# Measuring out projection work by each step's vector work, with a shorter DRAM round trip and a refilled weight ring

## The chip, the cores and the metric

The kernel runs on one core of a Trainium2 chip. The core has TensorE (matmuls; weight loads are shown on a line of their own, PEld), VectorE (DVE), ScalarE (ACT), GpSimd (POOL) and SyncE (SP), which run beside each other and wait for one another by semaphores. In this kernel SP and POOL mainly issue DMA transfers. The metric is the device time of one execution in microseconds; of several runs the median is given.

## The reference

One decoder layer for one sequence of 2048 tokens, 1024 wide, all in float32:

```python
h = rmsnorm(x, norm1_w)
proj = h @ w_in                                # 1024 x 3840
q_raw, f_raw, i_raw, g_raw = split(proj[..., :2048], 4)
o_hg = hgrn2(...)                              # 4 heads of 128: gated linear recurrence
rw_p = proj[..., 2048:]
rw_p = rw_p + (token_shift(rw_p) - rw_p) * mu
r, k, v, wd, ad, gd = split(rw_p, ...)
# RWKV-7, 8 heads of 64; the state S is 64 x 64 for each head:
#   sa = S a_t ;  S = S diag(w_t) + sa b_t^T + v_t k_t^T ;  y_t = S r_t
o_rw = groupnorm(y) * ln_w + ln_b + bonus, gated by g
x = x + concat([o_hg, o_rw], -1) @ w_out       # 1024 x 1024
u = causal_depthwise_conv3(rmsnorm(x, norm2_w) @ w_up) + conv_b     # 1024 x 5632
x = x + (silu(u[:2816]) * u[2816:]) @ w_down
return rmsnorm(x, final_norm_w)
```

Both recurrences run over the 2048 tokens. The kernel computes them in chunks of 64 tokens.

## The kernel before

**Arithmetic.** A large product is three matmuls on a value split into a high and a low part: high x high, high x low, low x high (`mm3`, L257 to L261). Each is 128x128 times 128x512. Splitting a weight is a cast on ScalarE (L243) and a subtraction on VectorE (L244).

**Two phases.** Phase 1 (`phase1`, L263 to L1085) has the input projection, both recurrences and the output projection of the first three of the four blocks of 512 tokens. Phase 2 (from L1088) has the output projection of the last block (accumulators `wacc`), then the FFN, whose two products are built from sums of blocks. The last matmuls of phase 1 and the first of phase 2 meet at what is called the seam. Phase 2 begins with loads on SP: three of convolution rows (`crow`, L1144 to L1146), then w_out and the recurrences' result `oT`, through the helper at L1153.

**Phase 1 is three streams.** Each is a Python generator that issues instructions and yields.

- `rw_stream`: RWKV-7 in eight super-steps (`rw_super`, L630 to L921), each of two head pairs over 512 tokens. In order: decays and keys; the masked products M (L706 to L709), a part of which makes a first round trip through DRAM (Ed, E, L715 to L725) that turns it so that each 32x32 triangle lies in one partition; transposes and `lv` (L757); the inversion of these triangles by elimination, 31 dependent steps of a multiply and an add on VectorE (L776, L778); a second round trip (L781 to L795), Ti and its transpose TiT to DRAM (T0d, T1d), then back as TZ and TTs; the matmuls that combine the halves, z (L802), z2 (L815), q (L828), g (L852, with adds at L855 and L858 that write AR), x (L868) and y (L875); the scan of the state, eight dependent steps of four small matmuls (L886) and a multiply on VectorE (L888); the output (L896 to L916) and the store of `oT` (L919).
- `hg_stream`: HGRN2 in sixteen units (`hg_unit`, L924 to L1046), among them the matmuls at L970 and L1012.
- `dense`: the list of projection jobs (L499 to L616). A "P" job is 128 columns for 512 tokens: eight k-steps of three matmuls with accumulator `pj`, each booked at 648 ns. There are 30 for each block. An "O" job is the output block of one of the blocks 0 to 2 (`out_block`, L367 to L401): four quarters of eight k-tiles; each k-tile loads and splits one 128x512 weight of w_out (`woraw`, on the POOL queue) and uses it for two booked units of 680 ns. Other jobs load and transpose rows (T, N) or make sums for phase 2 (E, W). The order is P of blocks 0 and 1, O of block 0, P of block 2, O of block 1, P of block 3, O of block 2.

**The pace.** The loop at L1078 takes one step of each recurrence and then calls `fill`, which draws projection units until the booked time is spent. That is a tick. TICK is 2000 ns for every tick, whatever the two steps hold:

```python
        while any(alive.values()):
            for key, g in (("r", rw_), ("h", hg_)):
                ...
            fill(TICK)
```

A unit that has to wait for a recurrence yields None, and the tick's credit is dropped. After the second round trip the RWKV stream yields twice (L796), so that two ticks of projection lie between it and L802. The list scheduler of the tile framework then places each engine's instructions by its own estimates and by the order in which they were issued.

**The weight ring.** Split weights lie in the buffers `wh` and `wl`, four of each. One P job takes two of each (k-tiles 0 to 3 and 4 to 7), one k-tile of an O job takes one of each. `load(i)` (L545) loads the weights of job i: for the first block raw from w_in, with split, and stores both parts to DRAM (Win); later blocks load the stored parts straight into wh and wl, by four DMAs on POOL (L558). At the head of each P job `load(i + 1)` (L596) issues the next job's load, whatever stands between the two.

Of the kernel before, what the change touches and what calls it, by code (L numbers as in the profile page):

```python
# [7 lines left out]
F32 = mybir.dt.float32  # L8
# [10 lines left out]
P = 128  # L19
T = 2048  # L20
D = 1024
KD = D // P
# [3 lines left out]
NFF = FF // P  # L26
TICK = 2000.0
NEG_C = -0.6065306597126334
# [30 lines left out]


@with_exitstack
def tile_layer(ctx, tc, consts, x, norm1_w, w_in, hg_lb_logits, hg_norm_w, rw_shift_mu, rw_w0, rw_w2,
# [3 lines left out]
    nc = tc.nc  # L66
    V, S, TE = nc.vector, nc.scalar, nc.tensor
    dma = nc.sync.dma_start
# [40 lines left out]
    def act(out_, in_, func, **kw):  # L109

        want = tables.get(func)
        if want is not None and want != tab["now"]:
            pre = S.preload_act_table_set(want)
            for u_ in tab["uses"]:
                tc.add_manual_dep(pre.ins, u_.ins.name, NOSYNC, reason="table order")
            tab.update(now=want, pre=pre, uses=[])
        i_ = S.activation(out_, in_, func, **kw)  # L117
        if want is not None:
            tc.add_manual_dep(i_.ins, tab["pre"].ins.name, NOSYNC, reason="table order")
            tab["uses"].append(i_)  # L120
        return i_
# [13 lines left out]
    with tc.tile_pool(name="vp", bufs=1, reuse_waits="tile") as vp, tc.tile_pool(name="ps0", bufs=1, space=PSUM, reuse_waits="tile") as pools["ps"]:  # L135
        rows = vp.tile([P, P], F32, name="rows")
        V.memset(rows, 0.0)
        n = 0
# [124 lines left out]
    def phase1(c1):  # L263
# [102 lines left out]

        def out_block(nb, oh=None, ol=None, then=None):  # L367


            for i2 in range(2):  # L370
                for dh in range(2):
                    accs = [bank("pj") for _ in range(2)]
                    for k in range(KD):
# [16 lines left out]
                        for q in range(2):  # L390
# [4 lines left out]
                            if i2 == 1 and dh == 1 and q == 1:  # L395
                                next_block(then, k)
                            yield 680
                    for q in range(2):
# [4 lines left out]
        rows = {}  # L403
# [95 lines left out]
        def dense():  # L499
# [64 lines left out]
            for n, jb in enumerate(jobs):  # L564
# [14 lines left out]
                if jb[0] in "OW":  # L579
                    while done["rw2"] < 2 * jb[1] + 2 or done["hg"] < 4 * jb[1] + 4:  # L580
                        yield None
                    if jb[0] == "W":
                        jb[2]()
                    else:
                        yield from (out_block(2, *rows["O"]) if jb[1] == 2 else out_block(jb[1], then=jb[1] + 2))
                    continue
# [5 lines left out]
                if i == 0:  # L592
                    next(ahead)
                    next(ahead)
                    constants()
                load(i + 1)  # L596
                i += 1
# [32 lines left out]
        def rw_super(nb, s_):  # L630
# [84 lines left out]
            Ed = dp.tile([64, 32, 32], F32, tag="Ed", name="Ed", bufs=2)  # L715
            T0d = dp.tile([2, 64, 32, 16], F32, tag="T0d", name="T0d", bufs=2)
            T1d = dp.tile([64, 16, 2, 32], F32, tag="T1d", name="T1d", bufs=2)
# [6 lines left out]
            for f in range(2):  # L724
                dma(E[64 * f:64 * f + 64], Ed)  # L725

            KBT = tile_("KBT", [2, 8, P], "KBT")
# [53 lines left out]
            TiT = rp.tile([P, 16, 32], F32, tag="E", name="TiT")  # L781
            dma(T0d.rearrange("f m t c -> (f m) t c"), Ti)
            act(TiT, Ti.rearrange("m a b -> m b a"), AF.Copy)
# [3 lines left out]
            for e in range(2):  # L787
                r0 = er0(e)
                for f in range(2):
                    dma(TZ[r0:r0 + 32, 0].rearrange("p u b h t -> p (u b h) t")[:, :, 16 * f:16 * f + 16],  # L790
                        T0d[f, 32 * e:32 * e + 16].rearrange("m t c -> t m c"))
                for q in range(2):
                    m0 = (e * 2 + q) * 16
                    dma(TTs[r0 + 32 * q:r0 + 32 * q + 32, :, 32 * q:32 * q + 32],
                        T1d[m0:m0 + 16].rearrange("m c f t -> (c f) m t"))  # L795
            for _ in range(2):  # L796
                yield
            z = bank2()
# [278 lines left out]

        while any(alive.values()):  # L1078
            for key, g in (("r", rw_), ("h", hg_)):
                if alive[key]:  # L1080
                    try:
                        next(g)
                    except StopIteration:
                        alive[key] = False
            fill(TICK)  # L1085

# [424 lines left out]
```

## Time and profile before

| | |
|---|---|
| runs | 2757.32, 2753.06, 2752.97 us; median 2753.06 |
| the profiled execution | 2757.5 us, of which the span is 2755.7 |
| mean granted TensorE clock in it | 0.983 |
| busy, share of the span | TensorE 96%, its weight loads 76%, VectorE 69%, ScalarE 49%, GpSimd 13% |
| projection matmuls (pj with wh, wl: 3 x 960) | 404.9, 380.6 and 380.6 us recorded; mean 397 to 422 ns of one |
| DMA | 515.78 MB, 187 GB/s on average |

The span runs from the first to the last record of the core; a part of the execution lies around it. The recorded durations of pipelined matmuls overlap (397 to 422 ns each), so they do not add up to time; how many end in a stretch does.

The lines below come from five views. The shares of the **chain of waits** follow the work that ended last backwards and say which engine or transfer it ran on. A **table by stretch** gives each engine's busy time in a window, with the granted clock, the busy share of the DMA engines and GB/s. A row of the **waits** says which engine and line waited (`PE pj L259`) for which engine and line (`ACT wh L243`), then the sum in us, the count and the longest. A **group** of instructions has a line, engine, operation, output<-input and count, then busy us, mean ns, and the idle time before them with what ended it. A **DMA row** ends with KB of one and the median us from issue to landing.

### The profile page before, as it was taken

What the parts mean: (1) busy time and instruction counts of PE and PEld (TensorE: products, weight loads), DVE (VectorE), ACT (ScalarE), POOL (GpSimd) and SP (SyncE); (2) the same over time, 40 slices, a digit from 0 to 9 for tenths busy, and PEclk for the clock granted to TensorE, in tenths of its full rate; (3) what the DMA queues carried; (4) which work ended last, traced back from release to release, by engine and by line L of the source; (5) the groups of instructions that cost most, each with busy time, mean ns of one, the idle gap of its engine ahead of it and who ended that gap; (6) DMA issues with size and microseconds to landing.
All of it is one profiled execution on the core that took longest, in us unless ns stands there. A gap on an engine that the chain in (4) does not pass through costs nothing.

```text
span 2755.7 us, 47958 instructions
## 1 busy us (share of the span) xinstructions
PE 2647.8 (96%) x18059; PEld 2107.5 (76%) x18059; DVE 1898.6 (69%) x3665; ACT 1350.4 (49%) x2164; POOL 368.3 (13%) x660
## 2 busy tenths in 40 slices
PE   7999999989999999999989999998999999999998
PEld 6777777767777767778667788886888888877887
DVE  4856556565456664657657889988997786667656
ACT  5546443444544444344446755455455555445444
POOL 6433222212321113222100000000000000000000
PEclk9999999999999999999999999999999999999999
DMA  8645544355663546844575367746662224999865
GB/s 301 202 152 166 165 138 131 115 146 173 217 176 104 152 146 203 286 138 123 161 273 160 114 205 258 242 148 218 223 228 77 88 85 144 327 327 313 285 196 184
DMA packets 364285, 515.78 MB, mean 187 GB/s; under 512 B 97311, under 2 KB 193941, under 8 KB 364053
## 3 DMA queue, kind: packets, MB, share of 16 engines
q1 hardware_dynamic: 312113, 343.29, 38.6%
q0 software_dynamic: 51872, 169.41, 18.9%
q8 instruction: 142, 2.33, 0.3%
q14 instruction: 90, 0.74, 0.1%
q10 hardware_dynamic: 68, 0.02, 0.0%
HBM read 375.22 MB, written 137.36 MB: 186 GB/s over the span
## 4 chain that ended last, share of the span: by engine, by line
PE 73%; DMA 8%; DVE 7%; issue 5%; ACT 4%; SPq 1%; POOL 1%; DVEq 0%; ACTq 0%; POOLq 0%
PE pj L259 8%; PE pj L260 7%; PE pj L261 7%; PE ua L261 5%; PE ua L259 5%; PE ua L260 5%; PE ud L259 3%; PE ud L260 3%; PE ud L261 3%; PE da L260 2%; PE da L261 2%; PE da L259 2%; PE hg L970 2%; PE db L259 2%; PE db L261 2%
## 5 line engine op out<-in xcount | busy, mean ns | idle before, releaser
L259 PE MATMUL pj<-hh,wh 128*128 128x512 f32 x960 | 404.9, 422 | 0.7 <-ACT hh L117 0.7
L261 PE MATMUL pj<-hh,wl 128*128 128x512 f32 x960 | 380.6, 397 | 0.0
L260 PE MATMUL pj<-hl,wh 128*128 128x512 f32 x960 | 380.6, 397 | 0.0
L259 PE MATMUL ua<-Bh,uwh 128*128 128x512 f32 x704 | 278.6, 396 | 13.8 <-ACT uwh L243 13.1
L261 PE MATMUL ua<-Bh,uwl 128*128 128x512 f32 x704 | 276.9, 394 | 0.9 <-DVE uwl L244 0.9
L260 PE MATMUL ua<-Bl,uwh 128*128 128x512 f32 x704 | 276.4, 393 | 0.0
L259 PEld LDWEIGHTS pj<-hh,wh 128*128 128x128 f32 x960 | 182.4, 190 | 54.2 <-issue 11.8
L260 PEld LDWEIGHTS pj<-hl,wh 128*128 128x128 f32 x960 | 182.6, 190 | 39.7 <-issue 6.2
L261 PEld LDWEIGHTS pj<-hh,wl 128*128 128x128 f32 x960 | 182.2, 190 | 40.1 <-issue 0.4
L243 ACT CAST uwh<-uraw 128x512 fp32r<-128x512 f32 x220 | 134.8, 618 | 145.9 <-PE ua L260 73.2
L243 ACT CAST dah<-draw 128x512 fp32r<-128x512 f32 x151 | 93.8, 621 | 184.1 <-PE da L260 50.5
L244 DVE TENSOR_TENSOR uwl<-uraw,uwh 128x512 fp32r<-128x512 f32 x220 | 146.7, 684 | 47.5 <-ACT uwh L243 47.3
L244 DVE TENSOR_TENSOR dal<-draw,dah 128x512 fp32r<-128x512 f32 x151 | 104.0, 689 | 107.3 <-ACT dah L243 107.2
L259 PEld LDWEIGHTS ua<-Bh,uwh 128*128 128x128 f32 x704 | 133.6, 190 | 43.1 <-ACT uwh L243 13.7
L261 PEld LDWEIGHTS ua<-Bh,uwl 128*128 128x128 f32 x704 | 133.5, 190 | 30.6 <-DVE uwl L244 2.7
L260 PEld LDWEIGHTS ua<-Bl,uwh 128*128 128x128 f32 x704 | 133.6, 190 | 27.3
L259 PE MATMUL ud<-Bh,uwh 128*128 128x512 f32 x352 | 137.9, 392 | 1.9 <-DVE cv L1362 1.9
L261 PE MATMUL ud<-Bh,uwl 128*128 128x512 f32 x352 | 137.1, 389 | 0.0
L260 PE MATMUL ud<-Bl,uwh 128*128 128x512 f32 x352 | 137.0, 389 | 0.0
L260 PE MATMUL da<-dbl,dah 128*128 128x512 f32 x340 | 133.8, 394 | 0.6 <-DVE dbl L244 0.5
L261 PE MATMUL da<-dbh,dal 128*128 128x512 f32 x340 | 133.3, 392 | 0.0
L259 PE MATMUL da<-dbh,dah 128*128 128x512 f32 x340 | 128.3, 391 | 2.4 <-ACT dbh L243 2.3
(558 smaller groups left out, 6036.7 us busy)
## 6 DMA issues: line engine op xcount, KB each, us to landing
uraw<-in_w_up_dram SPq DMA_DIRECT2D x176, 256.0 KB, 3.3
woraw<-in_w_out_dram POOLq DMA_DIRECT2D x96, 256.0 KB, 3.6
draw<-Sg SPq DMA_DIRECT2D x88, 256.0 KB, 3.1
draw<-Tw SPq DMA_DIRECT2D x88, 256.0 KB, 3.0
gd<-y SPq DMA_DIRECT2D x86, 256.0 KB, 2.9
xt<-x1d SPq DMA_DIRECT2D x32, 512.0 KB, 6.0
draw<-gd SPq DMA_DIRECT2D x63, 256.0 KB, 4.8
draw<-in_w_down_dram SPq DMA_DIRECT2D x63, 256.0 KB, 5.3
```

Source lines behind the costliest of these rows:

```text
L243: S.copy(hi, src)
L244: V.tensor_sub(lo, src, hi.bitcast(F32))
L259: TE.matmul(acc, lh, rh, start=first, stop=False, skip_group_check=skip)
L260: TE.matmul(acc, lh, rl, start=False, stop=False, skip_group_check=skip)
L261: TE.matmul(acc, ll, rh, start=False, stop=last, skip_group_check=skip)
L970: TE.matmul(o, kt[:, t0:t0 + 64], qs, start=True, stop=True, tile_position=(0, e * 64))
```

## The change

1. **Booking.** VectorE's engine object is wrapped (`Metered`): each of its operations adds 150 ns and 1.04 ns for each element of a row of its output to a counter; each ScalarE activation adds half of what it would be on VectorE. Each of the two round trips adds 8000.
2. **Pacing.** A tick's projection work is no longer 2000 ns but 900 ns and 0.45 of what the tick's two steps added to the counter. In place of two yields after the second round trip there is one.
3. **Round trip.** The DRAM buffer of Ti changes its layout, from (half, triangle, row, 16 columns) to (triangle, row, half, 16 columns). Its store becomes two DMAs in place of one, with runs of 64 bytes in DRAM; the loads of TZ become two in place of four. Both are issued ahead of the four loads of TTs, not among them.
4. **Ring.** The load of the next projection's weights is no longer issued at the head of the job ahead of an output block, but in the block, at the third last k-tile of its last quarter.

Lines of the recurrences lie about 30 lower in the new file. A VectorE operation that is called through the wrapper carries the wrapper's line there (L80).

```diff
-TICK = 2000.0
+FLOOR, RATE = 900.0, 0.45
+OP_NS, ELEM_NS, TRIP_NS = 150.0, 1.04, 8000.0
...
+class Metered:
+    def __init__(self, engine):
+        self.engine, self.ns = engine, 0.0
+    def __getattr__(self, name):
+        call = getattr(self.engine, name)
+        def f(out_, *args, **kw):
+            self.ns += OP_NS + ELEM_NS * width(out_)
+            return call(out_, *args, **kw)
+        return f
...
+    V = Metered(nc.vector)
...
+        V.ns += 0.5 * (OP_NS + ELEM_NS * width(out_))
         i_ = S.activation(out_, in_, func, **kw)
...
                             if i2 == 1 and dh == 1 and q == 1:
                                 next_block(then, k)
+                                if k == KD - 3 and last is not None:
+                                    last()
...
-                load(i + 1)
+                kinds = [jb_[0] for jb_ in jobs[n + 1:]]
+                if "O" not in kinds[:kinds.index("P") if "P" in kinds else 0]:
+                    load(i + 1)
...
-            T0d = dp.tile([2, 64, 32, 16], F32, tag="T0d", name="T0d", bufs=2)
+            T0d = dp.tile([64, 32, 2, 16], F32, tag="T0d", name="T0d", bufs=2)
...
             for f in range(2):
                 dma(E[64 * f:64 * f + 64], Ed)
+            V.ns += TRIP_NS
...
-            dma(T0d.rearrange("f m t c -> (f m) t c"), Ti)
+            for f in range(2):
+                dma(T0d[:, :, f, :], Ti[64 * f:64 * f + 64])
...
-                for f in range(2):
-                    dma(TZ[r0:r0 + 32, 0].rearrange("p u b h t -> p (u b h) t")[:, :, 16 * f:16 * f + 16],
-                        T0d[f, 32 * e:32 * e + 16].rearrange("m t c -> t m c"))
+                dma(TZ[r0:r0 + 32, 0].rearrange("p u b h t -> p (u b h) t"),
+                    T0d[32 * e:32 * e + 16].rearrange("m t f c -> t m (f c)"))
+            for e in range(2):
+                r0 = er0(e)
                 for q in range(2):
                     m0 = (e * 2 + q) * 16
                     dma(TTs[r0 + 32 * q:r0 + 32 * q + 32, :, 32 * q:32 * q + 32],
                         T1d[m0:m0 + 16].rearrange("m c f t -> (c f) m t"))
-            for _ in range(2):
-                yield
+            V.ns += TRIP_NS
+            yield
...
         while any(alive.values()):
+            t0 = V.ns
...
-            fill(TICK)
+            fill(FLOOR + RATE * (V.ns - t0))
```

More of the change, by code (lines that the diff above doesn't have):

```diff
@@ L58, in make_consts, with width @@
     return c
+def width(ap):
+    n = 1
+    for d in ap.shape[1:]:
+        n *= d
+    return n
+class Metered:
[7 more added lines that the diff above has]
+        return f
 @with_exitstack
@@ L66, in tile_layer @@
     nc = tc.nc
-    V, S, TE = nc.vector, nc.scalar, nc.tensor
+    S, TE = nc.scalar, nc.tensor
+    V = Metered(nc.vector)
     dma = nc.sync.dma_start
@@ L365, in mark, with out_block @@
             return f
-        def out_block(nb, oh=None, ol=None, then=None):
+        def out_block(nb, oh=None, ol=None, then=None, last=None):
             for i2 in range(2):
@@ L584, in dense @@
                     else:
-                        yield from (out_block(2, *rows["O"]) if jb[1] == 2 else out_block(jb[1], then=jb[1] + 2))
+                        yield from (out_block(2, *rows["O"]) if jb[1] == 2 else
+                                    out_block(jb[1], then=jb[1] + 2, last=lambda: load(i)))
                     continue
```

## The prediction

> **What bounds the kernel now.** I read the shares of the chain that ended last, then a table of busy time by stretch (its columns: busy us and instructions of TensorE, its weight loads, VectorE, ScalarE, GpSimd, then the granted clock), then TensorE's waits.
>
> ```profile
> PE 73%; DMA 8%; DVE 7%; issue 5%; ACT 4%; SPq 1%; POOL 1%; DVEq 0%; ACTq 0%; POOLq 0%
> ```
> ```profile
> 24.00:1390.00 1366.00, 1310.70 (x12231) 1014.62 (x12230) 829.54 (x2037) 621.83 (x994) 349.62 (x626) 0.98 0.53 167
> 1390.00:1398.00 8.00, 0.74 (x4) 0.32 (x3) 2.19 (x4) 1.24 (x2) 0.40 (x1) 0.69 0.76 265
> 1398.00:2755.70 1357.70, 1327.67 (x5802) 1086.71 (x5802) 1055.37 (x1594) 714.46 (x1141) 1.10 (x2) 0.99 0.62 205
> ...
> 2100.00:2150.00 50.00, 50.00 (x222) 41.40 (x221) 37.18 (x57) 24.68 (x37) 0.00 (x0) 1.00 0.29 94
> ```
> TensorE bounds it. The two long stretches are the two phases; the 8 us between them are the seam. The change touches the first phase: from the seam on, the order of the instructions on TensorE, ScalarE and SP is the same in both kernels. The first phase is idle on TensorE for 1366.0 - 1310.7 = 55.3 us, and runs at 0.98 of the clock. That is the whole prize; the number of matmuls does not change (13,917 TensorE instructions in either order). The last row gives the true price of a projection matmul: 50 / 222 = 0.225 us, so a unit of three is 0.68 us, close to the 648 ns that the planner books.
>
> ```profile
> PE pj L259 <- ACT wh L243: 14.7, 12, 4.3
> PE rw L802 <- DMA TZ<-T0d: 14.3, 9, 4.3
> ...
> PE rw L868 <- DVE AR L858: 8.9, 6, 2.2
> PE wacc L259 <- ACT Bh L236: 7.3, 1, 7.3
> PE hg L1012 <- DVE hk L1005: 3.9, 1, 3.9
> ```
> Two waits are aimed at: projection matmuls that wait for a split weight (14.7), and the inverse's matmuls at L802 that wait for the round trip through DRAM (14.3). The wait of 7.3 is the seam.
>
> ```profile
> 157.40:171.00 13.60, 13.60 (x181) 9.67 (x179) 6.43 (x18) 10.14 (x25) 2.33 (x4) 0.50 0.28 104
> ...
> sum 44.20, PE 39.04 PEld 28.63 DVE 21.36 ACT 21.27 POOL 6.30; mean PE 6.51 PEld 4.77 DVE 3.56 ACT 3.55 POOL 1.05
> ```
> This is the second cost of a wait. The row is the first of six stretches (at 157, 311, 598, 680, 960 and 1158 us; 13.6, 3.4, 13.6, 3.4, 6.8 and 3.4 long), the sum row all six, 44.2 us; in each the granted clock is one half. If every matmul in them went twice as fast, half of that, 22.1 us, would come back; that is the ceiling.
>
> **The change, part by part.**
>
> *The pace.* Before, each tick of the loop (one step of the RWKV stream, one of the HGRN stream) is followed by 2000 ns of projection work. After, by 900 ns plus 0.45 ns for each ns of vector work that the two steps are booked at. Walking the loop by hand gives the same 770 us of booked projection work in both, dealt out otherwise: about 1.0 to 1.8 us after a step of the state scan, 2.2 to 2.7 after a step of the elimination (L776, L778), over 5 after the ticks that send the two round trips. What it is dealt to is bound by VectorE:
>
> ```profile
> 110.00:140.60 30.60, 30.60 (x247) 25.29 (x247) 29.42 (x108) 10.33 (x19) 13.71 (x23) 1.00 0.58 192
> 1281.00:1315.60 34.60, 34.60 (x266) 28.54 (x266) 30.30 (x109) 14.02 (x24) 5.55 (x10) 1.00 0.28 90
> ```
> These are the first and the last elimination. VectorE is busy for 29.4 of 30.6 and 30.3 of 34.6 us, so TensorE reaches L802 too early and waits. Eight elimination ticks get some 0.5 us more each, and the trip one tick of 5.5 in place of two of 2.0: 8 x 0.5 + 1.5 = 5.5 us more cover, and the longest single wait is 4.3. The ordered list, however, has only slightly more projection between L757 and L802 than before (about +0.7 us on average, by counting matmuls at 0.225), because the scheduler places units by its own estimate; between the masks (L706) and L757 it has 3.5 us more, which covers the first trip. I take 14.3 to 4.3: **-10.0**, with bounds 0 and -14.3.
>
> *The shorter trip.* The store of Ti goes from one DMA of 128 rows to two of 2048 runs of 64 bytes; the loads of TZ from four to two, and no load of TTs stands before a load of TZ any more (before, the order was three TZ, two TTs, one TZ).
>
> ```profile
> T0d<-Ti SPq DMA_DIRECT2D x8, 256.0 KB, 2.1
> ...
> TTs<-T1d SPq DMA_DIRECT2D x32, 64.0 KB, 3.6
> ...
> TZ<-T0d SPq DMA_DIRECT2D x32, 32.0 KB, 2.8
> ```
> ```profile
> L790 SPq DMA_DIRECT2D TZ<-T0d x32: 397/499/2172, 144.3 to 1323.4; - x32
> ```
> SP saves two TZ issues at 0.5 and gets the last TZ out two TTs issues earlier, taken at the same 0.5: some 2.0 us. The store has four times the runs of a TZ load in each half. Below, it lands in 2.1 as now; above, time goes with the runs, 4 x 2.8 = 11.2, +9.1. A load of 512 runs costs 2.8 to 3.6 whatever its bytes, so most of that is fixed: I take +2, which cancels the 2.0. Net **0**, bounds -2 and +7 a trip, eight trips.
>
> [...] The rows agree that short runs are dear per byte: 64 KB of 128-byte runs (TTs) take 3.6, 256 KB in rows 2.1.
>
> *The weight ring.* Before, the next projection's weights sit in two of the four wh/wl buffers through a whole output block, so the block runs on two. After, they are loaded near its end.
>
> ```profile
> 594.00:680.00 86.00, 76.16 (x895) 54.70 (x894) 52.63 (x109) 39.01 (x66) 14.47 (x27) 0.92 0.51 155
> 680.00:950.00 270.00, 265.54 (x2221) 208.96 (x2220) 153.20 (x398) 121.61 (x193) 67.35 (x124) 0.99 0.52 163
> 950.00:1042.00 92.00, 79.97 (x912) 57.63 (x910) 55.56 (x114) 42.24 (x73) 15.09 (x29) 0.94 0.53 156
> ```
> ```profile
> woraw<-in_w_out_dram POOLq DMA_DIRECT2D x96, 256.0 KB, 3.6
> ```
> ```profile
> L243 ACT CAST wh<-woraw 128x512 fp32r<-128x512 f32 x96 | 58.9, 618 | 103.4 <-DMA woraw<-in_w_out_dram 52.6 <-PE pj L261 31.2 <-PE pj L260 9.9
> ```
> The first two output blocks idle 9.8 and 12.0 us; the 270 us between them, 4.5. With two buffers a split (0.62 on ScalarE, then VectorE) starts one weight (1.37 us of matmuls) ahead; with four, three weights. What stays: the four Win loads come ahead of the last woraw on the POOL queue and wait there for matmuls, then 3.6 to land and a split, so the last weight of each block can still be late by about 2; and the third output block never held the next weights. I take 14.7 to 4.7: **-10.0**, bounds 0 and -14.7.
>
> *The clock.* If these waits go, so do most of their half-clock stretches. Inside them many matmuls are small ones that wait for each other anyway: 181 in the first 13.6 us. I take half of the ceiling, rounded down: **-10**, bounds 0 and -22.1.
>
> [...]
>
> *The seam.* The projection runs out early: in the new order the last four scan steps (L886, L888), L896, L904 and L916 stand behind the last projection matmul. The first weight load of phase 2 stands on SP behind a load that now waits for the last scan step.
>
> ```profile
> 1357.87 0.28 DVE L888 TENSOR_TENSOR XH<-rw,WC 128x128 f32<-128x128 f32 x1
> ...
> 1358.70 0.29 DVE L888 TENSOR_TENSOR XH<-rw,WC 128x128 f32<-128x128 f32 x1
> ```
> ```profile
> 1378.70 1.72 PE rw L904 x4
> ...
> 1383.34 1.72 PE rw L916 x4
> ...
> 1390.32 0.24 PE pj L261
> ...
> 1391.81 0.65 SPq L1144
> ```
> The first two rows are one bare scan step, the others stand in the chain of waits. A step takes 1358.70 - 1357.87 = 0.83 us; four take 3.3. Before, the held load (L1144) starts 1391.81 - 1390.56 = 1.25 after the last projection matmul; after, some 3.7: +2.5. But L904 and L916, 1.72 each, move into the seam: -3.4. The rest of the last super-step is on ScalarE and VectorE, and its result is needed only by the last two of eight k-tiles, 6 x 12 x 0.225 = 16 us after the first. With more of the seam at half clock I take **+1**, bounds -3 and +14 (if the first matmul of phase 2 waited for all of it; that end is an estimate).
>
> *New waits.* The output blocks start in the elimination now: 66 of their units are dealt to elimination ticks of the fourth and sixth super-step, where VectorE is full; each pair carries a split. ScalarE gets 14 more table loads.
>
> ```profile
> L244 DVE TENSOR_TENSOR wl<-woraw,wh 128x512 fp32r<-128x512 f32 x96 | 65.9, 688 | 46.9 <-ACT wh L243 46.2 <-ACT hv L117 0.2
> ```
> ```profile
> L113 ACT ACT_TABLE_LOAD x42 | 53.9, 1283 | 0.7
> ```
> Splits: 33 x 0.69 = 22.8 us more for VectorE; TensorE's own longer stretch covers most. I take **+3** (0 to +22.8). Tables: 14 x 1.28 = 18 us on an engine busy for 622 of 1366; **+1** (0 to +18). The waits at L868 (8.9) and L1012 (3.9) stay: in the new order L868 still follows L852 with nothing between in six of eight super-steps. In the dearest case the scan gets less cover than 0.83 a step; single booked units of 0.65 nearly reach it: **0**, to +3.
>
> Sum: -10 - 10 + 0 - 10 + 1 + 3 + 1 = -25, from the profiled execution (2757.5; its span 2755.7 and 1.8 around it) to 2732.5. That execution lies 4.4 over the median of the runs, 2753.1, so the forecast for the median is **2728**.
>
> **The rivals.**
>
> *More comes back.* Waits and half clock go altogether: -14.3 - 14.7 - 22.1 = -51, to 2702. For: all three are in one phase and TensorE has nothing else to wait for. Against: the ordered list leaves L802 hardly more cover.
>
> *It cancels.* VectorE paces the elimination whatever TensorE is dealt, so the wait at L802 returns at another place; only the ring pays, half (-5), and the clock little: 2745 to 2751. For: VectorE's 29.4 of 30.6.
>
> *Slower by the store.* Time goes with runs, +9.1 a trip less the 2.0: +7.1, eight times, 57; of it the added cover takes 8 x 2 = 16. With the ring's -10: +31, to 2784. It decides where the store lands later than about 4 us after its issue. Against: 512 runs of 64 bytes, 2.8 in all.
>
> *Slower by VectorE.* The 22.8 us of splits are bare, since elimination fills VectorE; the ring's gain of 10 is set against them, the wait at L802 and the half clock stay, tables take 3 and the seam 1: -10 + 22.8 + 4 = +17, to 2770. It decides where VectorE's stretch in an output block outlasts TensorE's. Against: TensorE's stretch gets 5 us longer there too, and the HGRN work beside it is partly elsewhere.
>
> **How the numbers follow.** Forecast (2712 to 2743) 0.54; more comes back 0.13; it cancels 0.16; slower by the store 0.08; by VectorE 0.09. A measurement can tell 0.2%, 5.5 us, from no change: below 2747.6 is faster. Half of "it cancels" is: 0.54 + 0.13 + 0.08 = 0.75. Same takes the rest of it, 0.08; slower 0.17. The range takes in most of "more comes back" and leaves out the dearer parts of the two slower cases: 2700 to 2765; the forecast's own is 2712 to 2743.
>
> **What would show it.** Right: TensorE's wait at L802 below 6 us in all, at pj behind wh below 7; the windows of the output blocks idle below 6 each; fewer than 25 us at half clock before the seam; the seam 8 to 11 us. Wrong: T0d landing over 4 us after its issue; pj waiting for wl or wh inside the elimination; the wait at L802 near 14; a first matmul of phase 2 more than 12 us after the last projection matmul.

## The result and the profile after

Four runs of the changed kernel took 2774.41 to 2781.89 us, median **2780.52**; before, on the same chip, 2755.19. The ratio is **1.0084**, 95% interval 1.0068 to 1.0099: slower, by some 23 us, where 25 us faster was forecast. The profiled execution took 2779.57, its span is 2777.8: 22.1 more than before.

The table by stretch of the changed kernel, cut as in the prediction (first phase, seam, second phase):

```profile
24.00:1401.79 1377.79, 1305.56 (x12131) 1010.01 (x12129) 833.22 (x2030) 633.26 (x1002) 349.23 (x627) 0.97 0.54 166
1401.79:1415.69 13.90, 7.99 (x106) 4.51 (x105) 4.33 (x9) 7.08 (x9) 0.00 (x0) 1.00 0.57 196
1415.69:2777.80 1362.11, 1326.68 (x5802) 1084.62 (x5802) 1058.20 (x1597) 713.18 (x1141) 1.83 (x3) 0.99 0.62 204
```

The first phase ends 11.8 us later, although some 100 instructions of TensorE have left it for the seam; the seam is 13.9 in place of 8.0; the second phase, with the same order, takes 4.4 more, some 3 of it by its 200th matmul. Both traces hold 18,059 matmuls (the prediction's 13,917 stands in neither). TensorE's idle time in the first phase is 1377.8 - 1305.6 = 72.2, before 55.3. It should have fallen.

The chain that ended last is no help here: the profile follows it back over 37% of the span only (before, over nearly all of it).

```profile
PE 29%; DMA 3%; DVE 2%; issue 1%; SPq 1%; ACT 1%; DVEq 0%; ACTq 0%
```

TensorE's waits:

```profile
PE rw L836 <- DMA TZ<-T0d: 18.9, 6, 6.2
PE pj L285 <- ACT wh L269: 15.4, 17, 1.8
...
PE pj L456 <- ACT xt L143: 5.3, 6, 2.1
...
PE pj L285 <- DVE xh L80: 3.7, 4, 2.3
```

Both waits at which the change aims are longer than before (14.3 and 14.7). The third row is the transposes (T jobs) that come before their rows are ready, the fourth a projection that waits for VectorE to empty an accumulator; both were small.

Two sums over eight windows each show where TensorE idles: the eliminations (first to last operation of L776 or L778 on VectorE), then the stretches from there to the first z matmul. First before, then after; "sum" is the length, then each engine's busy time.

```profile
559.27:593.46 34.19, 33.33 (x255) 26.41 (x256) 30.84 (x110) 15.45 (x28) 7.09 (x13) 1.00 0.47 147
...
sum 254.97, PE 250.17 PEld 205.90 DVE 230.71 ACT 86.04 POOL 67.95; mean PE 31.27 PEld 25.74 DVE 28.84 ACT 10.76 POOL 8.49
...
sum 71.19, PE 58.33 PEld 40.54 DVE 33.62 ACT 43.98 POOL 20.43; mean PE 7.29 PEld 5.07 DVE 4.20 ACT 5.50 POOL 2.55
```
```profile
602.73:646.20 43.47, 38.24 (x295) 27.53 (x294) 37.95 (x117) 20.51 (x33) 10.69 (x20) 0.92 0.53 169
...
sum 286.92, PE 272.43 PEld 214.43 DVE 246.70 ACT 123.95 POOL 81.61; mean PE 34.05 PEld 26.80 DVE 30.84 ACT 15.49 POOL 10.20
...
sum 102.44, PE 75.00 PEld 55.75 DVE 60.88 ACT 36.46 POOL 26.40; mean PE 9.38 PEld 6.97 DVE 7.61 ACT 4.56 POOL 3.30
```

Idle in the eliminations: 4.8 before, 14.5 after. Between elimination and z: 12.9 before, 27.4 after; and these eight stretches last 102 us in place of 71. The first row of each fence is the fourth elimination. It starts 43 us later than before, and 1505 projection matmuls (accumulator `pj`) have started by then, before the change 1369: the recurrence has fallen back behind the projection that is dealt ahead of it. That shift is not yet a loss. At the fifth elimination the counts are 1920 and 1911, and the changed kernel is 2.9 us late; at the seventh (2825 and 2836) it is 4.6 us early. What separates the two executions comes after: 16.2 us from there to the last projection matmul, 6.3 at the seam, 4.2 in the second phase.

The DMA row of the new store, then the time for which SP itself was busy with one issue (min, median, max in ns): the T1d store before, the T0d store after, the T1d store after.

```profile
T0d<-Ti SPq DMA_DIRECT2D x16, 128.0 KB, 5.5
```
```profile
L785 SPq DMA_DIRECT2D T1d<-TiT x16: 544/614/1462, 141.8 to 1317.4; - x16
```
```profile
L815 SPq DMA_DIRECT2D T0d<-Ti x16: 544/557/4961, 140.9 to 1333.9; - x16
```
```profile
L818 SPq DMA_DIRECT2D T1d<-TiT x16: 666/1330/5130, 145.2 to 1336.6; - x16
```

The store lands in 5.5 us where it took 2.1 (in 3.9 and 3.3 in trip_only and ring_new_trip below). What is more, SP itself is busy longer: an issue behind the first half of the store took up to 5.1 us, where 1.5 was the most before, and the next ones start late.

```profile
140.86 4.29 SPq L815 DMA_DIRECT2D T0d<-Ti  x2
145.19 6.57 SPq L818 DMA_DIRECT2D T1d<-TiT  x2
152.83 1.16 SPq L822 DMA_DIRECT2D TZ<-T0d  x2
```

In this first trip (SP's timeline: start, length) the first TZ load starts 12.0 us after the elimination; before it was 3.8. Over the eight trips it starts 4.9 to 12.0 after, before 2.5 to 8.1.

ScalarE's timeline at the seam of the changed kernel:

```profile
1406.42 1.02 ACT L143 ACTIVATE yo<-rw 128x1024 f32<-128x1024 f32 x1 [8.51 <-PE rw L930]
1409.58 1.11 ACT L143 ACTIVATE yo<-rw,epsgn 128x1024 f32<-128x1024 f32 x1 [2.13 <-PE rw L938]
1410.72 1.06 ACT L143 ACTIVATE yo<-yo 128x1024 f32<-128x1024 f32 x1
1411.80 1.28 ACT L138 ACT_TABLE_LOAD   x1
1413.09 1.52 ACT L143 ACTIVATE yo<-yo,vt 128x512 f32<-128x512 f32 x2
1414.52 0.60 ACT L262 CAST woh<-Bl 128x512 fp32r<-128x512 f32 x1
```

The first cast of phase 2 stands behind the whole output of the last super-step on ScalarE. The load that it needs was issued at 1406.5; ScalarE comes to it at 1414.5. Before, that cast started 2.6 us after the issue of its load.

### The profile page after: what moved, and what is told of

It is laid out like the page before. It is cut to its first block, busy times and chain, and to the rows that moved or that the text cites. A ratio compares the mean times of both kernels' runs of the same rounds, so it can differ in the third digit from the quotient of the medians.

```text
span 2777.8 us, 47924 instructions
## 1 busy us (share of the span) xinstructions
PE 2647.6 (95%) x18059; PEld 2104.2 (76%) x18059; DVE 1906.9 (69%) x3665; ACT 1366.4 (49%) x2178; POOL 367.7 (13%) x660
## 3 DMA queue, kind: packets, MB, share of 16 engines
q0 software_dynamic: 51872, 169.41, 18.9%
## 5 line engine op out<-in xcount | busy, mean ns | idle before, releaser
L80 DVE TENSOR_TENSOR uwl<-uraw,uwh 128x512 fp32r<-128x512 f32 x220 | 146.7, 684 | 50.6 <-ACT uwh L269 50.6
L80 DVE TENSOR_TENSOR dal<-draw,dah 128x512 fp32r<-128x512 f32 x151 | 104.0, 689 | 102.1 <-ACT dah L269 101.9
L80 DVE SCALAR_TENSOR_TENSOR y<-cv,cvt,y 128x1024 f32<-128x1024 f32 x88 | 112.5, 1279 | 32.9 <-ACT y L143 32.8
```

Of the source, the lines that this page charges most:

```text
L80: return call(out_, *args, **kw)
```

## The experiments

The question was which of the three edits cost the time. **STORE**: the new store lengthens the trips. **ORDER**: dealing by vector work costs it, whatever the trips. All were timed in five rounds against the kernel before; ratios have 95% intervals.

**One edit alone, or one undone.** The edits are those of the diff above.

trip_only (kernel before with part 3 of the change):

> The kernel before with the new round trip alone (store of Ti in two DMAs of 64-byte runs, two TZ loads, TTs after them; the two yields and the 2000 ns ticks stay). Theory STORE (the new store makes each trip longer): in the changed kernel the first TZ load starts 4.9 to 12.0 us after the last elimination add, before 2.5 to 8.1, and the matmuls behind it start 3.9 us later on the mean of eight trips; with the old cover most of 8 x 3.9 = 31 is bare: +15 to +30, 2770 to 2785, and TensorE's wait behind TZ grows from 14 to over 30. Theory ORDER (the pacing's order costs the time, not the trip): within 5 of before, 2750 to 2760, the wait at TZ under 20.

Measured: **1.0021** (1.0008 to 1.0035), 2757.6. That is 4.9 over the median of before beside it: time and wait both lie inside ORDER's bounds, at their upper ends, and far from STORE's (a wait over 30). Still, the wait and the trips grew:

```profile
PE rw L804 <- DMA TZ<-T0d: 19.0, 8, 6.0
```
```profile
sum 96.30, PE 73.28 PEld 52.99 DVE 42.51 ACT 48.80 POOL 30.93; mean PE 9.16 PEld 6.62 DVE 5.31 ACT 6.10 POOL 3.87
```

Idle in the trips 96.3 - 73.3 = 23.0, 10 more than before.

ring_only (part 4):

> The kernel before with the weight ring alone (the next projection's weights are loaded near the end of the output block). Prediction's step: wait of pj behind wh from 14.7 to about 5, -10 with some half clock back: 2738 to 2748. Theory ORDER and theory STORE have no say in it. Against it stands the changed kernel's 15.4 for the same wait: if the ring does not help at all, 2753 to 2758 with the wait at 14 to 16.

Measured: **0.9976** (0.9965 to 0.9988), 2744.9. The ring pays. The wait at which it aims, then the first two output blocks, and the first phase with the sum of its half-clock stretches up to the seam:

```profile
PE pj L259 <- ACT wh L243: 8.5, 11, 2.8
```
```profile
561.90:668.00 106.10, 95.48 (x1048) 71.56 (x1046) 73.87 (x183) 53.23 (x89) 19.31 (x36) 0.95 0.50 158
919.00:1025.20 106.20, 94.83 (x1047) 72.00 (x1045) 71.69 (x177) 52.28 (x89) 19.29 (x36) 0.95 0.53 157
```
```profile
24.00:1376.94 1352.94, 1298.15 (x12232) 1006.96 (x12229) 828.43 (x2037) 622.09 (x994) 348.98 (x626) 0.99 0.53 168
...
sum 44.40, PE 37.56 PEld 27.77 DVE 26.02 ACT 16.89 POOL 5.27; mean PE 5.37 PEld 3.97 DVE 3.72 ACT 2.41 POOL 0.75
```

The wait fell from 14.7 to 8.5, but the blocks idle 10.6 and 11.4, much as before, and the phase 54.8 (before 55.3): other waits grew, L868's for AR from 8.9 to 12.0. In these two executions the half clock fell as well: 44.4 us, by the same count 68.3 before (eleven stretches, the one that runs into the second phase among them). TensorE was busy in 58.0 of those before and in 37.6 here: (58.0 - 37.6) / 2 = 10 us. The half is an estimate: in such a stretch projection matmuls start 0.43 us apart (before, 1157.9 to 1160.4 us), and the prediction's 0.225 is at the full clock. The fall is not the ring's doing, as far as the runs tell: the profiled execution of ring_only is the shortest of its twelve (2739.5), and the mean granted clock is 0.986 over these twelve and 0.986 over the 23 of the kernel before beside them.

pace_only (parts 1 and 2):

> The kernel before with booking and pacing alone (900 ns + 0.45 of the booked vector work, 8000 for each trip, one yield; round trip and ring as before). Theory STORE: the old store lands in 2 us, the cover for the trip is there, so no slower than before but for the seam, which grows from 7.6 to some 14 with 4 us moved into it: 2750 to 2762. Theory ORDER: the loss is here, 2770 to 2780.

Measured: **1.0120** (1.0101 to 1.0139), 2781.7: ORDER, just above its range. The profiled execution is the longest of five, 2791.2. Its first phase idles 1392.58 - 1316.36 = 76.2, the seam is 14.1:

```profile
24.00:1416.58 1392.58, 1316.36 (x12127) 1012.36 (x12126) 832.30 (x2027) 631.65 (x1000) 347.68 (x624) 0.97 0.52 163
1416.58:1430.71 14.13, 8.47 (x107) 4.61 (x105) 5.45 (x10) 8.39 (x11) 0.55 (x1) 1.00 0.62 211
```

after_old_trip (changed kernel without part 3):

> The changed kernel with the round trip of before (one store of 128 rows, four TZ loads among the TTs loads; pacing, one yield and ring as changed). Theory STORE: 15 to 25 of the loss of 25 come back, 2755 to 2766, and the wait behind TZ falls from 18.9 to under 8. Theory ORDER: 2775 to 2782.

Measured: **1.0079** (1.0059 to 1.0099), 2772.9: 2 under ORDER's range, 7 over STORE's. STORE is out as the main cause.

**Which part of the pace.** Four kernels on after_old_trip or beside it. In these expectations EVEN is the theory that steps with little vector work are starved, TRIP that the projection booked for the trips is missed elsewhere, TAIL that only the bare end costs, VECTOR that projection in a full elimination waits for VectorE.

trips_1890 (V counts nothing, FLOOR is 1890):

> after_old_trip (changed pace and ring, old round trip, 1.0079 of before) with the booking of vector work taken out: 1890 ns after every tick and 0.45 x 8000 more at each of the two trips; projection then lasts to the end of the recurrences. Theory EVEN (the loss comes from ticks that get little projection since they hold little vector work): about as ring_only, 2742 to 2752, the waits behind ScalarE in the recurrence fall from 12 in pace_only to under 5. Theory TRIP (58 us of projection booked for the sixteen trips is missed elsewhere): still slow, 2765 to 2775. Theory TAIL (only the end, where projection has run out): about 6 to 9 below after_old_trip, 2764 to 2768.

Measured: **1.0026** (1.0008 to 1.0044).

vec_975 (no TRIP_NS, two yields, FLOOR is 975):

> after_old_trip with the vector work booked at 0.45 as there, but nothing for the trips and two yields as before; the floor is 975 ns so that projection lasts to the end. Theory EVEN: the loss stays, 2765 to 2780. Theory TRIP: gone, 2742 to 2752, or a little more for the missing cover at TZ. Theory TAIL: 2762 to 2768.

Measured: **1.0054** (1.0034 to 1.0074).

late_790 (FLOOR is 790):

> after_old_trip with the floor at 790 ns in place of 900, so that the projection lasts until the last three ticks. Theory TAIL: the seam falls from 14.5 to about 8 and what was moved out of the first phase (about 4) goes back into it: 6 to 9 of the loss come back for certain, and under this theory nearly all the loss, 2750 to 2766. Theory EVEN: ticks with little vector work get 0.11 less still, so the seam's gain is offset: 2768 to 2778.

Measured: **1.0066** (1.0041 to 1.0090). None of the three theories holds alone: EVEN fails in trips_1890, TRIP in vec_975, TAIL in late_790. Against ring_only's 0.9976, the trips' booking alone costs 0.50% and the vector work's 0.78%, where both together cost 1.03%; the end of the projection costs little.

elim_2000:

```diff
-            fill(FLOOR + RATE * (V.ns - t0))
+            fill(2000.0 if V.flat else FLOOR + RATE * (V.ns - t0))   # V.flat: in the elimination
```

> after_old_trip (2772.9, 1.0079) with 2000 ns, as before the change, in the ticks of the elimination; all other ticks keep the changed pace, and the projection lasts to the third last tick. Theory VECTOR (more projection in the elimination waits for a full VectorE: TensorE's idle time in the eight eliminations is 4.8 before and 17.8 in after_old_trip, 12.2 of it in the two that now hold half an output block; and the early end of the projection bares the seam): idle in the eliminations below 8, the seam below 10, 10 to 18 back, 2755 to 2763. Theory TRIP (the booked trips take the time): 2768 to 2775, since they are booked as before.

Measured: **1.0080** (1.0056 to 1.0103). Its eliminations, then its trips:

```profile
sum 270.78, PE 262.25 PEld 213.05 DVE 245.14 ACT 120.42 POOL 74.40; mean PE 32.78 PEld 26.63 DVE 30.64 ACT 15.05 POOL 9.30
...
sum 78.05, PE 60.02 PEld 43.72 DVE 41.96 ACT 34.95 POOL 24.13; mean PE 7.50 PEld 5.46 DVE 5.24 ACT 4.37 POOL 3.02
```

Idle in the eliminations fell to 8.5 and the seam to 6.7, about as VECTOR wanted, and the time did not move: 2775.0, the end of TRIP's range. The trips idle 18.0, though they are booked 5.5 us of cover; TensorE is busy in them for 60.0, before 58.3. The first phase as a whole idles 65.5, after_old_trip 69.6, and the half clock took more than that difference. Its stretches up to the second phase (TensorE is busy in 55.8 us of them in after_old_trip):

```profile
sum 78.53, PE 73.53 PEld 55.96 DVE 39.31 ACT 26.09 POOL 7.27; mean PE 5.25 PEld 4.00 DVE 2.81 ACT 1.86 POOL 0.52
```

(73.5 - 55.8) / 2 = 9 us, in the profiled executions; over six runs each the mean clock is 0.9837 and 0.9805. The waits move; VECTOR as the whole cause falls.

**The order of the loads, and the layout by itself.** ring_tz_first (ring_only, with the four TZ loads in a loop ahead of the four TTs loads, layout of before):

> ring_only (0.9976 of before) with the four loads of TZ ahead of the four of TTs, in the layout of before. The last TZ load leaves SP two TTs issues earlier, 1 to 2 us a trip. If TensorE's wait behind TZ (9.2 in ring_only) is set by it: 4 to 8 us below ring_only, 2736 to 2742. If the VectorE chain sets the recurrence's pace and the wait only moves: within 3 of ring_only, 2742 to 2750.

Measured: **0.9943** (0.9924 to 0.9961), 2736.4: faster than both kernels. Its first phase and half-clock sum:

```profile
24.00:1367.15 1343.15, 1295.46 (x12230) 1006.78 (x12228) 829.44 (x2037) 621.64 (x994) 349.58 (x626) 0.99 0.54 170
...
sum 40.95, PE 32.52 PEld 25.57 DVE 20.92 ACT 13.69 POOL 5.08; mean PE 4.65 PEld 3.65 DVE 2.99 ACT 1.96 POOL 0.72
```

Idle 47.7, 7.6 less than before. (This execution is the shortest of its eight, 2730.2.)

ring_new_trip (ring_only with part 3 of the change):

> The kernel before with the ring and the whole new round trip, pace as before. Against ring_tz_first (0.9943 of before) only the layout differs: the store in 64-byte runs and two TZ loads in place of four. Theory STORE: the first TZ load starts 5 to 10 us after the elimination in place of 2.5 to 6; TensorE's idle time between elimination and z rises from 10 to 20 or more, 10 to 20 above ring_tz_first: 0.998 to 1.002 of before, 2747 to 2757. If the layout costs nothing and only the order counts: 0.993 to 0.996, 2733 to 2742.

Measured: **1.0015** (1.0002 to 1.0028). Only the layout differs from ring_tz_first: the store of 64-byte runs with its two loads costs 0.72%, 20 us. STORE is right about its own edit: the first TZ load starts 4.8 to 10.5 us after the elimination, in ring_tz_first 2.5 to 6.2.

tz_first_only (kernel before, TZ loads first):

> The kernel before with nothing but the order of the TZ loads. Additive with the ring (0.9976 alone, 0.9943 with it): 0.9967, 2743. If the order works only where the ring is refilled: 0.999 to 1.001.

Measured: **0.9969** (0.9957 to 0.9982); additive with the ring. TensorE's wait behind TZ is 8.4, before 14.3.

after_tz_first (after_old_trip, TZ loads first):

> after_old_trip (1.0079; changed pace and ring, store and loads in the layout of before) with the four TZ loads ahead of the TTs loads. If the last TZ load's way through SP is what the paced kernels lose between elimination and z: idle time there from 18.0 to about 10 and 8 to 16 back, 2752 to 2762. If the pace loses its time in many places: 0 to 6 back, 2763 to 2772.

Measured: **1.0043** (1.0028 to 1.0058): 10 back. In its trace the idle time in the trips did not fall (22.3, after_old_trip 18.0), so the gain is not seen in that wait.

**Is it the dealing, or any shift?**

tick_1890 and tick_2050 (ring_tz_first, TICK alone):

> ring_tz_first (0.9943) with an even 1890 ns in place of 2000 after every tick. Theory CHANCE (any other place of the projection among the steps of the recurrence costs 10 to 20 us): 2746 to 2760. Theory MEASURED (it is the dealing by vector work that costs): within 6 of ring_tz_first, 2732 to 2744, a little longer since the projection then outlasts the recurrences.

> ring_tz_first (0.9943) with an even 2050 ns. Theory CHANCE: 2746 to 2760. Theory MEASURED: within 6 of ring_tz_first, 2732 to 2744, the seam a little dearer since the projection ends earlier.

Measured: **0.9945** (0.9923 to 0.9966) and **1.0009** (0.9992 to 1.0025). A slower even pace costs nothing, one 2.5% faster costs 0.66%, 18 us. So a loss of this size does not need dealing by vector work. The first phase and half-clock sum of tick_2050:

```profile
24.00:1394.57 1370.57, 1306.52 (x12233) 1015.58 (x12231) 832.00 (x2036) 630.29 (x1000) 349.29 (x625) 0.98 0.54 166
...
sum 75.06, PE 62.69 PEld 48.64 DVE 33.17 ACT 28.51 POOL 7.19; mean PE 6.27 PEld 4.86 DVE 3.32 ACT 2.85 POOL 0.72
```

Against ring_tz_first it idles 16.4 more (64.1), and (62.7 - 32.5) / 2 = 15 more go to half clock; the two executions lie 30 apart, the medians less. Only 6 of the 16.4 lie in eliminations and trips. Half lies in the third output block, ring_tz_first, then tick_2050:

```profile
1280.50:1367.20 86.70, 82.72 (x957) 63.12 (x956) 58.36 (x143) 41.92 (x74) 15.25 (x29) 0.98 0.51 152
```
```profile
1291.80:1394.60 102.80, 91.07 (x957) 69.67 (x955) 57.92 (x143) 42.74 (x74) 14.53 (x27) 0.87 0.45 128
```

So the loss is of the same size as a good part of the changed pace's, but not in the same stages.

**The splits of the output blocks.** In out_block, with `wl` made on another engine, or not at all:

```diff
-                        wh, wl = split(wp, raw, [P, 512], "w", 4)
+                        S.copy(wh, raw)                 # wh, wl: tiles as in split
+                        nc.gpsimd.tensor_sub(wl, raw, wh.bitcast(F32))     # best_pool
+                        wl = wh                         # the three kernels with no_low
```

> after_old_trip with one part left out: the low part of the output projection's weights in phase 1 is not made (96 subtractions of 0.69 us on VectorE); the matmuls take the high part in its place, so their count stays. Theory VECTOR, as the cause in the two eliminations that hold output blocks: their idle time falls from 12.2 to below 5 and 8 to 15 come back, 2758 to 2765. If the cast on ScalarE or the load is what TensorE waits for: within 5, 2768 to 2778.

> ring_tz_first (0.9943) with the low part of the output projection's weights in phase 1 made on GpSimd in place of VectorE. If the three output blocks, idle for 24 us in all there, wait for VectorE's queue: 5 to 12 below ring_tz_first, 0.990 to 0.993, 2724 to 2733. If they wait for the cast on ScalarE or the load: within 4 of it. If GpSimd takes much longer than the 0.69 us of VectorE or holds back the weight loads that it issues: above it, 0.996 or more.

> ring_tz_first with one part left out: the low part of the output projection's weights in phase 1 is not made, the high part stands in its place in the matmuls. Theory PLACE (the subtractions cost where an output block stands in an elimination, which here holds only 12 of the 96 splits): 0 to 5 us below ring_tz_first, 0.9925 to 0.9943. Theory WORK (66 us less on VectorE is worth 12 us wherever it stands): 0.989 to 0.991.

> tick_2050 (1.0009) with the same part left out. Theory PLACE: of the 18 us between it and ring_tz_first 8 to 16 come back, 0.995 to 0.998. Theory WORK: 12 us as well, 0.996 to 0.997, and then best_no_low gains as much. If the splits have no say in what tick_2050 lost (the round trip and the half clock): under 4 us, 0.9995 or more.

Measured: no_low_after **1.0034** (1.0019 to 1.0049), best_pool **1.0115** (1.0094 to 1.0136), best_no_low **0.9886** (0.9862 to 0.9911), tick_2050_no_low **0.9932** (0.9908 to 0.9957). Leaving the low part out is worth 12 us in the changed pace, 16 in ring_tz_first, 21 in tick_2050: the work costs wherever it stands. That it costs more inside an elimination (PLACE) is not shown. In no_low_after the two eliminations with output blocks idle 7.6, before that edit 12.2: not below 5, as VECTOR had it.

## Why the prediction was wrong

Kernels that differ by one edit give a sum (in us of 2755; the first difference carries some 3, the others 6 to 7):

| from, to | edit | ratios | us |
|---|---|---|---|
| before, ring_only | ring | 1, 0.9976 | -6.6 |
| ring_only, ring_tz_first | order of the TZ loads | 0.9976, 0.9943 | -9.1 |
| ring_tz_first, after_tz_first | booking and pace | 0.9943, 1.0043 | +27.6 |
| after_tz_first, changed kernel | layout of T0d | 1.0043, 1.0084 | +11.3 |
| | | sum | +23.2 |

The sum closes by construction, and each row depends on what else is changed. Between other neighbours the ring gives -2 to -11, the order -8.5 and -10, booking and pace +19 to +33, the layout +14 and +20.

**The pace: -10 forecast, +28 measured.** This step failed, and in its sign. It took the booked 5.5 us for cover of a 4.3 us wait. But its own next sentence had the ordered list, which held only 0.7 us more there. The traces side with the list: with the old round trip, TensorE has 59 to 62 us of work in the trips of the paced kernels (after_tz_first, elim_2000, after_old_trip) and 58 to 63 in those of the even ones (before, ring_tz_first, ring_only). The wait at L802 was to fall to 4.3; it is 14.0 in after_tz_first and 18.9 in the changed kernel. And the step priced only the wait that was to go, not what 770 us of projection dealt out anew do to every other step: the waits at transposes and accumulators, the eliminations. Where the time went: from ring_tz_first to after_tz_first, the idle time of the first phase grows from 47.7 to 68.5. All of that lies in two stages, the eliminations (3.7 to 17.0) and the trips (10.1 to 22.3), here as sums of ring_tz_first, then of after_tz_first:

```profile
sum 259.00, PE 255.26 PEld 209.92 DVE 235.50 ACT 90.58 POOL 65.92; mean PE 31.91 PEld 26.24 DVE 29.44 ACT 11.32 POOL 8.24
sum 71.30, PE 61.18 PEld 43.67 DVE 34.83 ACT 43.41 POOL 20.95; mean PE 7.65 PEld 5.46 DVE 4.35 ACT 5.43 POOL 2.62
```
```profile
sum 283.87, PE 266.92 PEld 209.81 DVE 247.01 ACT 120.35 POOL 81.14; mean PE 33.36 PEld 26.23 DVE 30.88 ACT 15.04 POOL 10.14
sum 81.39, PE 59.06 PEld 44.14 DVE 48.20 ACT 29.53 POOL 24.17; mean PE 7.38 PEld 5.52 DVE 6.02 ACT 3.69 POOL 3.02
```

The seam takes 7 more, and the half clock some 12 in these two executions. "It cancels" named the returning wait, and priced it at nothing.

**The trip: 0 forecast; +6 measured alone, +11 beside the ring, +1 in the changed kernel.** Of the 2.0 us a trip that were to be saved, 1.0 was for the order (two TTs issues at 0.5). That was right: the order is worth 8.5 to 10 us, 1.1 to 1.2 a trip. The other 1.0 (two TZ issues fewer) and the +2 for the store make +1 a trip, +8, for the layout; it costs +11 to +20, 1.4 to 2.5 a trip. The landing was sized about right at the old pace (3.3 and 3.9 in place of 2.1; 5.5 in the changed kernel). What the step left out is that SP is busy with the issues behind the store (one took up to 5.1 us in the changed kernel, 3.4 in trip_only and in ring_new_trip), so that the loads start late; the rows of SP's issues before (T1d's store: 1.5 us at most) did not have it. In ring_new_trip the first TZ load starts 3.1 us later than in ring_tz_first, on the mean of eight trips; the landing is only 1.3 longer. That short runs are dear per byte, which the prediction had from its rows, the runs show as well: 128 KB in 64-byte runs took 5.5 us to landing, 256 KB in rows 2.1. The rival "slower by the store" named 2784, near the result, but not by its cause: the layout's +11 is less than half of the loss.

**The ring: -10 forecast, -6.6 measured; right in sign, too large in size.** At the even pace of 2000 ns the wait behind wh is 14.7, 14.2 and 11.6 without the ring (before, tz_first_only, trip_only) and 8.5, 10.1 and 10.2 with it (ring_only, ring_tz_first, ring_new_trip): some 4 us less, where 10 were forecast. The windows of the output blocks, which were to idle below 6 each, idle 10.6 and 11.4 in ring_only, 10.4 and 10.4 in the changed kernel:

```profile
559.10:650.70 91.60, 81.20 (x593) 62.21 (x591) 70.61 (x183) 45.80 (x71) 19.27 (x36) 0.94 0.57 169
929.50:1030.30 100.80, 90.43 (x1012) 66.97 (x1011) 73.58 (x200) 46.47 (x82) 18.19 (x34) 0.97 0.53 154
```

Two more buffers shorten one wait in the blocks and others take its place; best_no_low, which makes no low part, idles 13.4 in the first two blocks, ring_tz_first 20.3, so the making of the weights holds a part. In the changed kernel the wait behind wh is 15.4, in pace_only 16.2: there the pace made it long again. Where the rest of the ring's 6.6 us comes from is not shown.

**The clock: -10 forecast, about +5 in the changed kernel.** Its half-clock stretches up to the second phase, with the one that runs into it, are 78.5 us, TensorE busy in 68.3 of them, before 68.3 and 58.0:

```profile
1178.02:1191.67 13.65, 9.49 (x86) 6.74 (x87) 4.54 (x14) 1.57 (x4) 1.61 (x3) 0.50 0.60 136
...
sum 78.50, PE 68.29 PEld 51.27 DVE 33.98 ACT 19.09 POOL 12.80; mean PE 5.25 PEld 3.94 DVE 2.61 ACT 1.47 POOL 0.98
```

(68.3 - 58.0) / 2 = 5. The four runs have a mean clock of 0.982, the kernel before 0.985 to 0.986 beside the experiments; 0.003 x 2755 = 8 us is the most that this is worth, an estimate. Right was that half clock follows waits, wrong that the waits would go. In the profiled execution of tick_2050 (+15) it is as large a term as the idle time itself (+16.4). The half-clock stretches of the two kernels last 3.4, 6.8, 10.2 or 13.7 us. In the 3.4 us ahead of each of the twelve in the first phase of the changed kernel, TensorE is busy for up to 1.85 us, in sum for 17.1 of 40.9, where it is busy for 1305.6 of 1377.8 in the whole phase; ahead of the eleven of before, for up to 1.82, in sum for 12.6 of 37.5. The changed kernel's:

```profile
986.88:990.29 3.41, 1.85 (x20) 1.14 (x20) 1.97 (x5) 0.76 (x2) 0.05 (x1) 1.00 1.12 229
...
sum 40.92, PE 17.05 PEld 12.06 DVE 23.42 ACT 17.39 POOL 7.19; mean PE 1.42 PEld 1.01 DVE 1.95 ACT 1.45 POOL 0.60
```

**The seam: +1 forecast; it is 5.9 longer**, of which the moved L904 and L916 (3.4) and four scan steps (3.3) are work that left the first phase. The forecast had credited the 3.4; in its own terms the seam costs 5.9 - 3.4 = +2.5, and the second phase takes 4.4 more, which it did not have. The step looked for the delay on SP. SP's loads were in time; the casts wait on ScalarE behind the last super-step's activations (the first starts at 1414.5, 8.0 after the issue of its load, before 2.6), and "its result is needed only by the last two k-tiles" does not help an instruction that stands ahead in the same queue.

**New waits: +4 forecast.** The waits of projection matmuls behind VectorE and of the transposes come to 11 and 5 us, where 2 and 2 stood; the eliminations, two of which now hold splits, have 14.5 - 4.8 = 10 us more idle time, but elim_2000 shows that this alone does not set the total.

**Range.** Of the upper ends listed with the terms, +22.8 for splits and +7 a trip went to one rival each and +14 at the seam to none; 2765 left no room for two at once, and the pace had no upper end above zero. Of the signs that were to show the forecast right, none came: the waits are 18.9 and 15.4, the blocks idle 10.4, the seam is 13.9, and 71.7 us lie at half clock before it.

**What stays open.** Why the pace costs 28 us is not settled. The idle time that it adds to the first phase lies in the eliminations and the trips, but taking it out of the eliminations gave no time back (elim_2000), and neither did the later end of the projection (late_790); each part of the booking costs by itself; an even pace 2.5% too fast costs 18. What the slow kernels have in common in the traces is that the projection runs ahead of the recurrence: the fourth elimination starts at 602.7 in the changed kernel and 572.2 in tick_2050, at 551.4 in ring_tz_first and 547.9 in tick_1890. Counted in projection matmuls that have started by then:

| loads of TZ | kernel: matmuls, ratio |
|---|---|
| old order | ring_only: 1369, 0.9976; trips_1890: 1386, 1.0026; late_790: 1471, 1.0066; vec_975: 1482, 1.0054; elim_2000: 1488, 1.0080; after_old_trip: 1512, 1.0079 |
| TZ first | tick_1890: 1355, 0.9945; ring_tz_first: 1369, 0.9943; tick_2050: 1396, 1.0009; after_tz_first: 1512, 1.0043 |

Within the intervals, the time grows with the lead in both rows, though not in proportion: the first 17 to 27 matmuls cost 14 to 18 us, the 116 to 126 after them 9 to 15. The lead is gone by the fifth elimination, and most of the loss comes later: against ring_tz_first the changed kernel is 16 us behind at the seventh elimination and 49 at the end. That the lead is the cause is argued, not shown: no run put the lead back and kept the booking.

## What to carry to other kernels

Cover that is booked in a planner is not cover in the engines' order: count the instructions between producer and consumer in the ordered list, and price the change by that. The store in short runs cost its landing (5.5 us in place of 2.1) and also the engine that issues it (up to 5.1 us for one issue); try the order of the loads first, which here gave 9 us for nothing. Test an even pace a little faster and slower before a cleverer one: the kernel's sensitivity to it was as large as all that was to be gained, and the two plain edits (ring and order) gave 0.9943. A profile shows one execution: before a difference of 10 us between two profiles is put down to an edit, compare how far the runs of one kernel lie apart.

## What the runs showed of the hardware

- Behind the store in two DMAs of 2048 runs of 64 bytes, one issue of T1d's store took SP 1.3 us at the median and up to 5.1 (the row of L818); behind the store in 128 rows, 0.6 and up to 1.5 (the row of L785).
- GpSimd took 1.43 us on the mean for a 128x512 subtraction (group of best_pool) that VectorE did in 0.69 in the kernel before (L244, wl<-woraw), and best_pool lost 1.7% against ring_tz_first:

```profile
L387 POOL TENSOR_TENSOR wl<-woraw,wh 128x512 fp32r<-128x512 f32 x96 | 137.0, 1431 | 123.2 <-ACT wh L386 116.0 <-DMA T1d<-TiT 5.5 <-PE rw L825 1.1
```

- TensorE was at half clock for 33 us (ring_tz_first) to 74 us (elim_2000) of its busy time up to the start of the second phase, in kernels with 18,059 matmuls each; its idle time in the first phase was 47.7 and 65.5 us there.
